# Column halves in the chunk products, transposed rows scaled once, decays made by ScalarE

## The chip, the cores and the metric

The kernel runs on one core of a Trainium2 chip. The metric is the device time of one execution in microseconds (us), lower is better. The core's engines run side by side and wait for one another through semaphores: TensorE (PE, with its weight loads shown apart as PEld), VectorE (DVE), ScalarE (ACT), GpSimd (POOL) and SyncE (SP), which here issues nearly all DMAs. PE multiplies a stationary operand (weights, `lhsT`) with a moving one and writes to banks of PSUM; DVE and ACT read these banks, POOL works on SBUF alone.

## The reference, cut to what matters

512 rows of 1024 features pass through one Mamba-2 layer, one differential attention layer and a last normalisation, all in float32. The change lies almost wholly in the first layer:

```python
h = rms_norm(x, norm_g)
zxbcdt = h @ w_in                       # z (2048), x/B/C (4096), dt (32 heads)
xbc = silu(causal_depthwise_conv(xbc, conv_w, conv_b))
dt = softplus(dt_raw + dt_bias)
a = -exp(a_log)
...
acs = cumsum(a * dt)                    # per chunk and head
seg = acs[:, :, None] - acs[:, None, :]
decay = exp(where(causal, seg, -inf))
cb = einsum("blgn,bsgn->blsg", c_c, b_c)
y_diag = einsum("blsgr,bsgrp->blgrp", cb[..., None] * decay, x_c)
y_off = einsum("blgn,bgrpn->blgrp", c_c, state) * exp(acs)
...
x = x + gated_group_rms_norm(y, z, g) @ w_out
```

There are 8 groups with 4 heads each, a head has 64 features and the state 128.

## The kernel before

**Numbers.** The large projections are made in three products of fp32r: a value is split into a head (`hi`) and a rest (`lo`), and `mm3` (L227) adds hi·hi, hi·lo and lo·hi. The gains of the norms are multiplied into the weights as they are split: ACT writes `whi` (`head`, L137), DVE `wlo` (`rest`, L143). Weights come in segments of 1 MB into `raw` (two buffers), and `whi` and `wlo` have two buffers each. The order of the segments is `order_a`, then `ORDER_B`.

**The first norm** is taken apart. The transposed rows `x_t` are split as they come (`split_x`, L356) into `hh`/`hl` ("a_hi", "a_lo" in the trace); the factor 1/rms of each row is applied later. `squares` and `scales` (L289, L294) make it as a column `r_col` (one value a row of x, for results with rows on partitions) and as a row `r_row` (copied along all partitions by a matmul of a matrix of ones with four diagonal matrices, which POOL makes). `z_out` (L344) scales by the column inside the Silu; `conv` (L471) multiplies the bank by `r_row` on DVE before its four taps.

**The groups.** For group g, `group_proj` (L485) makes four banks (B, C and two of x, 96 records of PE), each followed by `conv`: one ACT tap, three DVE taps, a Silu on ACT. `decays` (L532) fetches the cumulated sums `acs` in a DMA that repeats them over partitions, subtracts a column (POOL), fills the entries above the diagonal (POOL, `affine_select`) and takes the exponential (ACT). `ssd` (L552) makes the scores `pcb` of the group, multiplies them into the decays of each head (DVE, L582), and from these the output inside chunks `pyd` (L605: per chunk and head, `dec` as weights of 128 columns, `xdt` with 64 columns as the moving side, plain fp32), then the part from the states, gate, norm and transposes. Chunks are 128 long here.

**The order.** A planner orders the instructions of each engine by its own estimate of times, not by the order of the text. Where `Ordered.on` is set (T, A and V stand for PE, ACT and DVE), each instruction is pinned behind the one written before it on its engine. Before the change this is so for ACT and DVE in the first four tiles (L366 to L371) and in the second layer (from L687). Dense projections come from generators (`stream_a`, `stream_b`), and `until` (L281) draws from them until a step is done; so PE has projections to lay beside the chunk work.

**The end** (L986 and on) is written out by hand: the last head's transposes and gates (`gate_head`), the last projection (`rows`, L902), and residual adds put into the bank of an unfinished sum (`add_in`, L941), after which PE goes on adding to that bank.

```python
            for c in (2 * q, 2 * q + 1):
                for h in range(R):
                    o = (c % 2) * 256 + h * HD
                    T.matmul(pyd[q][:, o:o + HD], lhsT=dec[:, h, c, :], rhs=xdt[:, c, h, :], start=True, stop=True)
```

Of the kernel before, what the change touches and what calls it, by code (L numbers as in the profile page):

```python
# [17 lines left out]
P = 128  # L18
# [43 lines left out]
def trunk(ctx, tc, x, x_t, par, w_dt, w_in, w_out, w_kvqg, w_bo, d_skip, lam_qk, fin_g, out):  # L62
# [59 lines left out]
    def load(i):  # L122
# [165 lines left out]

# [5 lines left out]
    def scales(tag, ss):  # L294
# [67 lines left out]
    A.activation(begin, ident[:, 0:1], AF.Copy)  # L362
    first = load(0)()
# [7 lines left out]
    V.on = A.on = False  # L371
# [13 lines left out]
    V.tensor_scalar(out=sg1, in0=prm[:, C_SG:C_SG + 1], scalar1=0.5 * (1.0 - LAM0), scalar2=None, op0=ALU.mult)  # L385
    dtw_raw = sm.tile([P, KD, H], F32, name="dtw_raw")
    nc.sync.dma_start(dtw_raw[:], w_dt)
# [10 lines left out]
    for k in range(KD):  # L398
        w = dw[:, k].rearrange("p a b h -> p (a b h)")
        T.matmul(ps_dt, lhsT=w, rhs=hh[:, k, :], start=k == 0, stop=False)  # L400
        T.matmul(ps_dt, lhsT=w, rhs=hl[:, k, :], start=False, stop=k == KD - 1)

    pre = sm.tile([P, P], F32, name="pre")
    for c in range(NQ):
        sl, hi, lo = (slice(i * H, (i + 1) * H) for i in (c, 0, 1))
        cs = slice(c * P, (c + 1) * P)
        A.copy(pre[sl, :], ps_dt[lo, cs])
        V.tensor_tensor(out=pre[sl, :], in0=ps_dt[hi, cs], in1=pre[sl, :], op=ALU.add)
# [3 lines left out]
    V.tensor_scalar(out=pre, in0=pre, scalar1=prm[:, C_DTB:C_DTB + 1], scalar2=None, op0=ALU.add)  # L412
    e1 = sm.tile([P, P], F32, name="e1")
# [57 lines left out]
    def conv(ps, ft, name, bufs):  # L471
# [3 lines left out]

        u = ps
        V.tensor_tensor(out=u, in0=ps, in1=r_row, op=ALU.mult)
        A.activation(xc, u, AF.Identity, scale=cw[3], bias=prc[:, ft:ft + 1])
        for k in (2, 1, 0):
            d = 3 - k  # L480
            V.scalar_tensor_tensor(out=xc[:, d:], in0=u[:, :S - d], scalar=cw[k], in1=xc[:, d:], op0=ALU.mult, op1=ALU.add)
# [50 lines left out]
    def decays(j):  # L532

        for g in (2 * j, 2 * j + 1):
# [5 lines left out]
            GP.tensor_copy(een, dec[:, :, 1:3, P - 1])  # L540
            for h in range(R):
                GP.tensor_tensor(out=dec[:, h], in0=dec[:, h], in1=acs_tok[:, :, R * g + h].unsqueeze(2).to_broadcast([P, NQ, P]), op=ALU.subtract)
                GP.affine_select(out=dec[:, h], in_=dec[:, h], compare_op=ALU.is_ge, fill=-BIG, base=0,
                                 pattern=[[0, NQ], [1, P]], channel_multiplier=-1)
            decs[g] = (dec, een)
        for g in (2 * j, 2 * j + 1):
            dec, een = decs[g]
            A.activation(een, een, AF.Exp)
            for h in range(0, R, 2):
                A.activation(dec[:, h:h + 2], dec[:, h:h + 2], AF.Exp)  # L550

    def ssd(g):  # L552
# [28 lines left out]
        for h in range(R):  # L581
            V.tensor_tensor(out=dec[:, h], in0=dec[:, h], in1=pcb.rearrange("p (c l) -> p c l", l=P), op=ALU.mult)  # L582
# [319 lines left out]
    def rows():  # L902
        ws = {0: use_b(("c", 2, 0), 1, 2)}
        for t, n, hs in ((0, 0, (4, 5)), (1, 0, (4, 5)), (0, 1, (4, 5)), (1, 1, (4, 5)),
# [17 lines left out]
            elif (t, n, hs) == (2, 0, (6,)):  # L922
                add_in(t, n)
# [78 lines left out]
    gate_head(h, 0, 2)  # L1002
    turn(h, 2)
# [115 lines left out]
```

## Time and profile before

| what | us |
|---|---|
| time, median of 3 runs (lowest to highest) | 736.55 (736.23 to 737.25) |
| the profiled execution's own time | 736.51 |
| its span, first to last instruction | 734.7 |
| records of PE | 3733 |
| first record of PE starts, last one ends | 1.5, 728.1 |
| POOL busy | 114.8 |
| loads of ACT's function tables | 33, 42.3 busy |

A record is one instruction of an engine. An fp32 matmul shows as two records of PE, an fp32r one as one. Ends of PE's records are modelled, and records overlap: the distance between starts is what a record costs in a dense stretch. In rows of groups, the columns are engine, operation, tiles (written <- read), count, and lowest, middle and highest duration in ns, then first and last start; rows of the timeline give start, length, engine, line, operation, tiles, count, and in brackets the idle time before and what ended it. "L53" is the line of the helper through which PE, ACT and DVE are called, so tiles tell the instructions apart.

### The profile page before, as it was taken

The numbers are of one execution on the slowest core, as the hardware profiler recorded it, in microseconds if no ns is written. First come the engines' busy times: TensorE is split into PE (matmuls) and PEld (weight loads), VectorE is DVE, ScalarE is ACT, GpSimd is POOL, SyncE is SP. The second block draws the span as 40 slices with busy tenths as digits, with TensorE's granted clock in tenths as the row PEclk, the third lists the DMA queues.
The fourth block names the chain that finished last, engine by engine and source line by source line (L and its number), as shares of the span: only waits on it lengthen the run. The fifth ranks groups of instructions, "written<-read, shape, count | busy, mean of one in ns | idle before, by whom it ended". The sixth has DMA issues, their size and how long they took to land.

```text
span 734.7 us, 10327 instructions
## 1 busy us (share of the span) xinstructions
PE 723.1 (98%) x3733; PEld 605.0 (82%) x3733; DVE 530.8 (72%) x1202; ACT 445.3 (61%) x975; POOL 114.8 (16%) x158
## 2 busy tenths in 40 slices
PE   9999999999999999999999999999999999999996
PEld 7788878888887888877888879888898898889874
DVE  5679955798568669469895655666757857785886
ACT  6849672864829356256433258766766766766566
POOL 0117231402233141150110201000000000000002
PEclk9999999999999999999999999999999999999999
DMA  8552313224132233132113220331221131122003
GB/s 314 215 193 97 128 45 116 78 95 172 59 114 65 108 115 116 58 116 102 71 58 114 87 86 8 115 115 58 65 109 57 58 116 58 58 80 93 29 1 114
DMA packets 12914, 70.83 MB, mean 96 GB/s; under 512 B 1728, under 2 KB 2496, under 8 KB 5312
## 3 DMA queue, kind: packets, MB, share of 16 engines
q1 hardware_dynamic: 12576, 69.90, 26.5%
q8 instruction: 29, 0.48, 0.3%
q10 hardware_dynamic: 288, 0.28, 0.1%
q14 instruction: 21, 0.17, 0.1%
HBM read 68.02 MB, written 2.16 MB: 96 GB/s over the span
## 4 chain that ended last, share of the span: by engine, by line
PE 86%; DVE 6%; ACT 5%; issue 1%; DMA 1%; POOL 0%; ACTq 0%; POOLq 0%; SPq 0%
PE pg L53 20%; PE po L53 13%; PE pz L53 10%; PE pt L53 7%; PE pv L53 6%; PE pq L53 6%; PE pk L53 6%; PE pyd L53 4%; PE pb L53 3%; PE sc L53 3%; PE pc L53 2%; DVE wlo L53 2%; ACT L53 1%; PE pyt L53 1%; PE pxt L53 1%
## 5 line engine op out<-in xcount | busy, mean ns | idle before, releaser
L53 DVE SCALAR_TENSOR_TENSOR wlo<-raw,prm,whi 128x512 fp32r<-128x512 f32 (+1 forms) x256 | 151.4, 640 | 49.6 <-ACT whi L53 49.2
L53 ACT ACTIVATE whi<-raw,prm 128x512 fp32r<-128x512 f32 (+1 forms) x256 | 137.1, 609 | 58.5 <-PE pz L53 12.4
L53 PE MATMUL pg<-a_hi,whi 128*128 128x512 f32 x256 | 102.4, 401 | 0.4 <-DVE xc L53 0.4
L53 PE MATMUL pg<-a_hi,wlo 128*128 128x512 f32 x256 | 102.7, 404 | 0.0
L53 PE MATMUL pg<-a_lo,whi 128*128 128x512 f32 x256 | 101.4, 397 | 0.0
L53 DVE SCALAR_TENSOR_TENSOR xc<-pg,prc,xc 128x511 f32<-128x511 f32 (+2 forms) x96 | 70.0, 743 | 4.4 <-ACT xc L53 3.6
L53 PEld LDWEIGHTS pg<-a_hi,whi 128*128 128x128 f32 x256 | 48.2, 188 | 11.4 <-issue 0.8
L53 PEld LDWEIGHTS pg<-a_hi,wlo 128*128 128x128 f32 x256 | 48.1, 188 | 11.0
L53 PEld LDWEIGHTS pg<-a_lo,whi 128*128 128x128 f32 x256 | 48.2, 188 | 10.8
L53 PE MATMUL po<-whi,yh 128*128 128x512 f32 x128 | 50.9, 400 | 0.7 <-ACT yh L53 0.6
L53 PE MATMUL po<-wlo,yh 128*128 128x512 f32 x128 | 50.9, 400 | 0.4 <-DVE wlo L53 0.4
L53 PE MATMUL pz<-wlo,a_hi 128*128 128x512 f32 x128 | 50.5, 401 | 0.0
L53 PE MATMUL pz<-whi,a_lo 128*128 128x512 f32 x128 | 50.1, 399 | 0.0
L53 PE MATMUL po<-whi,yl 128*128 128x512 f32 x128 | 49.9, 396 | 0.0
L53 PE MATMUL pz<-whi,a_hi 128*128 128x512 f32 x128 | 49.6, 400 | 0.0
L53 ACT ACT_TABLE_LOAD x33 | 42.3, 1283 | 9.5 <-DVE xc L53 7.9
L957 POOL TENSOR_TENSOR ot<-ot,fg 128x512 f32<-128x512 f32 x4 | 5.1, 1285 | 257.6 <-PE pc L53 256.4
L53 ACT ACTIVATE s<-s,mx 128x128 f32<-128x128 f32 (+3 forms) x64 | 35.6, 559 | 9.5 <-DVE mx L53 9.3
L580 POOL TENSOR_TENSOR xe<-xdt,tok 128x256 f32<-128x256 f32 x24 | 15.4, 672 | 152.5 <-DVE xdt L53 152.5
L53 DVE CUSTOM_DVE_ANT_0 s<-sc,bias 128x128 f32<-128x128 f32 (+3 forms) x64 | 29.4, 488 | 12.3 <-PE sc L53 11.9
L53 PE MATMUL pv<-whi,b_hi 128*128 128x256 f32 x128 | 36.6, 286 | 0.0
L53 ACT ACTIVATE tmp<-dx 128x256 f32<-128x256 f32 x32 | 13.1, 411 | 38.0 <-DVE dx L53 38.0
(244 smaller groups left out, 1749.1 us busy)
## 6 DMA issues: line engine op xcount, KB each, us to landing
raw<-in_w_in SPq DMA_DIRECT2D x23, 1024.0 KB, 4.9
raw<-in_w_kvqg SPq DMA_DIRECT2D x16, 1024.0 KB, 4.8
dec<-acs_d SPq DMA_DIRECT2D x8, 1024.0 KB, 4.8
raw<-in_w_out SPq DMA_DIRECT2D x8, 1024.0 KB, 4.7
raw<-in_w_bo SPq DMA_DIRECT2D x4, 1024.0 KB, 4.8
x_tok<-in_x SPq DMA_DIRECT2D x4, 512.0 KB, 9.4
out<-ot SPq DMA_DIRECT2D x7, 256.0 KB, 2.4
raw<-in_w_in SPq DMA_DIRECT2D x4, 256.0 KB, 5.4
```

What stands on the lines that cost most here:

```text
L53: i = op(*args, **kw)
L580: GP.tensor_tensor(out=xe[:, c], in0=xdt[:, c], in1=toe_tok[:, c, hs].unsqueeze(2).to_broadcast([P, R, HD]), op=ALU.mult)
L957: GP.tensor_tensor(out=o, in0=o, in1=f, op=ALU.mult)
```

## The change

It has six parts, and computes the same outputs.

1. `pyd`: each matmul becomes two, each with 64 columns of `dec` as weights, writing partitions 0 to 63 and 64 to 127 of the bank.
2. The row of 1/rms stays in its PSUM bank. Once z0 has used the unscaled `hh`/`hl`, `xt` is multiplied by it in place and split anew (`scale_x`, `head_x`, `rest_x`); `conv` loses its multiplication, and `z_out` scales by the column for j = 0 only. The four diagonal matrices are made by DVE.
3. From the first product of z0 up to the last of `rest_x`, the order on ACT and DVE is that of the text; on PE from the first product to z0's last. The dt product moves ahead of z0's second half, `dtw_raw` is fetched where `prc` was, and `prc` later.
4. Decays: for each head and chunk, ACT takes Relu(column - value), then exp(-...), so that entries above the diagonal become 1; the exponentials of the last values (`een`) are read straight from the fetched tile.
5. The scores' bank `pcb` is multiplied by a lower triangle of ones (DVE, `ones` masked once on POOL), which takes the entries above the diagonal out.
6. At the end, `add_in(2, 0)` comes after `gate_head(h, 0, 2)`, and `add_in(3, 1)` inside `gate_head(h, 3, 4)`, ahead of its last subtraction.

```diff
@@ load
-            nc.sync.dma_start(prc[:], par[:, C_CB:N_PAR])
+            nc.sync.dma_start(dtw_raw[:], w_dt)
@@ scales
-        V.tensor_copy(col, rsqrt(ss, NT, "y"))
         w = small.tile([P, NT + 1, P], F32, tag="wide", name=f"{tag}diag", bufs=2)
         GP.memset(w[:, NT], 1.0)
+        V.tensor_copy(col, rsqrt(ss, NT, "y"))
         for t in range(NT):
-            GP.tensor_tensor(out=w[:, t], in0=ident, in1=col[:, t:t + 1].to_broadcast([P, P]), op=ALU.mult)
+            V.tensor_scalar(out=w[:, t], in0=ident, scalar1=col[:, t:t + 1], scalar2=None, op0=ALU.mult)
         ps = long_bank(f"{tag}ps_r")
-        T.matmul(ps, lhsT=w[:, NT], rhs=w[:, 0:NT].rearrange("p t n -> p (t n)"), start=True, stop=True)
-        row = res.tile([P, S], F32, tag="r_row", name=f"{tag}r_row")
-        A.copy(row, ps)
+
+        def row():
+            T.matmul(ps, lhsT=w[:, NT], rhs=w[:, 0:NT].rearrange("p t n -> p (t n)"), start=True, stop=True)
+            return ps
+
         return col, row
@@ z_out
-        A.activation(zs, ps, AF.Silu, scale=r_col[:, t:t + 1])
+        A.activation(zs, ps, AF.Silu, scale=1.0 if j else r_col[:, t:t + 1])
@@ start
-    V.on = A.on = False
+    T.on = True
     for k in range(4):
         for t in range(NT):
             tk = slice(t * P, (t + 1) * P)
             mm3(pz0[t], (hh[:, k, tk], hl[:, k, tk]), (wh[:, k, :], wl[:, k, :]), k == 0, False)
     for k in range(4, KD):
         split_x(k)
-    fetch(2)
+    second = load(1)()
     for t in range(NT):
         nc.sync.dma_start(x_tok[:, t, :], x[t * P:(t + 1) * P, :])
-    ss = sm.tile([P, NT], F32, name="ass")
-    for t in range(NT):
-        squares(ss, t)
-    r_col, r_row = scales("a", ss)
...
-    dtw_raw = sm.tile([P, KD, H], F32, name="dtw_raw")
-    nc.sync.dma_start(dtw_raw[:], w_dt)
+    third = load(2)()
+    nc.sync.dma_start(prc[:], par[:, C_CB:N_PAR])
...
         T.matmul(ps_dt, lhsT=w, rhs=hl[:, k, :], start=False, stop=k == KD - 1)
+    for piece in second:
+        lay(piece)
+    ss = sm.tile([P, NT], F32, name="ass")
+    for t in range(NT):
+        squares(ss, t)
 
     pre = sm.tile([P, P], F32, name="pre")
     for c in range(NQ):
...
+        A.copy(pre[c * H:(c + 1) * H, :], ps_dt[H:2 * H, c * P:(c + 1) * P])
+    r_col, row = scales("a", ss)
+
+    def scale_x(k):
+        V.tensor_tensor(out=xt[k // 2][:, k % 2, :], in0=xt[k // 2][:, k % 2, :], in1=r_row, op=ALU.mult)
+
+    def head_x(k):
+        A.copy(hh[:, k, :], xt[k // 2][:, k % 2, :])
+
+    def rest_x(k):
+        V.tensor_tensor(out=hl[:, k, :], in0=xt[k // 2][:, k % 2, :], in1=hh[:, k, :].bitcast(F32), op=ALU.subtract)
+
+    w0 = ready.pop(("z", 0, 1))
+    for t in range(2):
+        run(tok_mm(pz0[t], t, 1, w0))
+    r_row = row()
+    for t in range(2, NT):
+        run(tok_mm(pz0[t], t, 1, w0))
+    z_out(0, 0, pz0[0])
+    (h0, l0, _), (h1, l1, _), (h2, l2, _), (h3, l3, _) = third
+    h0(0), l0(0), h1(1)
+    scale_x(0), head_x(0), l1(1), scale_x(1)
+    h2(2), rest_x(0), z_out(0, 1, pz0[1])
+    head_x(1), scale_x(2), h3(3), rest_x(1)
+    head_x(2), l2(2), scale_x(3), z_out(0, 2, pz0[2])
+    head_x(3), rest_x(2), l3(3), rest_x(3), z_out(0, 3, pz0[3])
+    T.on = False
...
+    for k in range(4, KD):
+        scale_x(k)
+        head_x(k)
+        if k > 4:
+            rest_x(k - 1)
+    rest_x(KD - 1)
+    V.on = A.on = False
...
+    GP.affine_select(out=ones, in_=ones, compare_op=ALU.is_ge, fill=0.0, base=0, pattern=[[1, P]], channel_multiplier=-1)
...
-    w0 = use(("z", 0, 1))
-    for t in range(NT):
-        run(tok_mm(pz0[t], t, 1, w0))
-        z_out(0, t, pz0[t])
@@ conv
-        u = ps
-        V.tensor_tensor(out=u, in0=ps, in1=r_row, op=ALU.mult)
-        A.activation(xc, u, AF.Identity, scale=cw[3], bias=prc[:, ft:ft + 1])
+        A.activation(xc, ps, AF.Identity, scale=cw[3], bias=prc[:, ft:ft + 1])
@@ decays
-            GP.tensor_copy(een, dec[:, :, 1:3, P - 1])
+            A.activation(een, dec[:, :, 1:3, P - 1], AF.Exp)
             for h in range(R):
-                GP.tensor_tensor(out=dec[:, h], in0=dec[:, h], in1=acs_tok[:, :, R * g + h].unsqueeze(2).to_broadcast([P, NQ, P]), op=ALU.subtract)
-                GP.affine_select(out=dec[:, h], in_=dec[:, h], compare_op=ALU.is_ge, fill=-BIG, base=0,
-                                 pattern=[[0, NQ], [1, P]], channel_multiplier=-1)
+                for c in range(NQ):
+                    A.activation(dec[:, h, c, :], dec[:, h, c, :], AF.Relu, scale=-1.0, bias=acs_tok[:, c, R * g + h:R * g + h + 1])
+            for h in range(0, R, 2):
+                A.activation(dec[:, h:h + 2], dec[:, h:h + 2], AF.Exp, scale=-1.0)
             decs[g] = (dec, een)
...
@@ ssd
+        pcv = pcb.rearrange("p (c l) -> p c l", l=P)
+        V.tensor_tensor(out=pcv, in0=pcv, in1=ones.unsqueeze(1).to_broadcast([P, NQ, P]), op=ALU.mult)
...
-                    T.matmul(pyd[q][:, o:o + HD], lhsT=dec[:, h, c, :], rhs=xdt[:, c, h, :], start=True, stop=True)
+                    for r in (slice(0, 64), slice(64, 128)):
+                        T.matmul(pyd[q][r, o:o + HD], lhsT=dec[:, h, c, r], rhs=xdt[:, c, h, :], start=True, stop=True)
@@ end
-            elif (t, n, hs) == (2, 0, (6,)):
-                add_in(t, n)
...
     gate_head(h, 0, 2)
+    until((2, 0, 6))
+    add_in(2, 0)
     turn(h, 2)
...
-    gate_head(h, 3, 4)
+    def between():
+        until((3, 1, 5))
+        add_in(3, 1)
+
+    gate_head(h, 3, 4, between)
     square_in(2, 1)
-    until((3, 1, 5))
     rest2 = last_root(2)
     scale(1, 0, r1)
-    add_in(3, 1)
```

More of the change, by code (lines that the diff above doesn't have):

```diff
@@ L362, in trunk @@
     A.activation(begin, ident[:, 0:1], AF.Copy)
+    dtw_raw = sm.tile([P, KD, H], F32, name="dtw_raw")
     first = load(0)()
@@ L401, in trunk @@
         T.matmul(ps_dt, lhsT=w, rhs=hl[:, k, :], start=False, stop=k == KD - 1)
+    for piece in second:
[3 more added lines that the diff above has]
+        squares(ss, t)
     pre = sm.tile([P, P], F32, name="pre")
     for c in range(NQ):
[L405 to L408, printed above, removed]
+        A.copy(pre[c * H:(c + 1) * H, :], ps_dt[H:2 * H, c * P:(c + 1) * P])
[22 more added lines that the diff above has]
+    for c in range(NQ):
+        sl = slice(c * H, (c + 1) * H)
+        V.tensor_tensor(out=pre[sl, :], in0=ps_dt[0:H, c * P:(c + 1) * P], in1=pre[sl, :], op=ALU.add)
     for c in range(NQ):
@@ L412, in trunk @@
     V.tensor_scalar(out=pre, in0=pre, scalar1=prm[:, C_DTB:C_DTB + 1], scalar2=None, op0=ALU.add)
+    for k in range(4, KD):
[5 more added lines that the diff above has]
+    V.on = A.on = False
+    V.tensor_scalar(out=sg1, in0=prm[:, C_SG:C_SG + 1], scalar1=0.5 * (1.0 - LAM0), scalar2=None, op0=ALU.mult)
     e1 = sm.tile([P, P], F32, name="e1")
@@ L474, in conv @@
         cw = [prc[:, at + k:at + k + 1] for k in range(4)]
-        u = ps
-        V.tensor_tensor(out=u, in0=ps, in1=r_row, op=ALU.mult)
-        A.activation(xc, u, AF.Identity, scale=cw[3], bias=prc[:, ft:ft + 1])
+        A.activation(xc, ps, AF.Identity, scale=cw[3], bias=prc[:, ft:ft + 1])
         for k in (2, 1, 0):
             d = 3 - k
-            V.scalar_tensor_tensor(out=xc[:, d:], in0=u[:, :S - d], scalar=cw[k], in1=xc[:, d:], op0=ALU.mult, op1=ALU.add)
+            V.scalar_tensor_tensor(out=xc[:, d:], in0=ps[:, :S - d], scalar=cw[k], in1=xc[:, d:], op0=ALU.mult, op1=ALU.add)
         A.activation(xc, xc, AF.Silu)
@@ L539, in decays @@
             een = small.tile([P, R, 2], F32, tag="een", name=f"een{g}")
-            GP.tensor_copy(een, dec[:, :, 1:3, P - 1])
+            A.activation(een, dec[:, :, 1:3, P - 1], AF.Exp)
             for h in range(R):
-                GP.tensor_tensor(out=dec[:, h], in0=dec[:, h], in1=acs_tok[:, :, R * g + h].unsqueeze(2).to_broadcast([P, NQ, P]), op=ALU.subtract)
-                GP.affine_select(out=dec[:, h], in_=dec[:, h], compare_op=ALU.is_ge, fill=-BIG, base=0,
-                                 pattern=[[0, NQ], [1, P]], channel_multiplier=-1)
+                for c in range(NQ):
+                    A.activation(dec[:, h, c, :], dec[:, h, c, :], AF.Relu, scale=-1.0, bias=acs_tok[:, c, R * g + h:R * g + h + 1])
+            for h in range(0, R, 2):
+                A.activation(dec[:, h:h + 2], dec[:, h:h + 2], AF.Exp, scale=-1.0)
             decs[g] = (dec, een)
[L546 to L550, printed above, removed]
     def ssd(g):
@@ L581, in ssd @@
         for h in range(R):
-            V.tensor_tensor(out=dec[:, h], in0=dec[:, h], in1=pcb.rearrange("p (c l) -> p c l", l=P), op=ALU.mult)
+            V.tensor_tensor(out=dec[:, h], in0=dec[:, h], in1=pcv, op=ALU.mult)
         hst = bp.tile([P, 3, R, HD], F32, tag="hst", name=f"hst{g}")
```

1 line of the change is left out of this document (removed).

## The prediction

> **What bounds the kernel now.** I read the page's busy shares first, then the chain of work that ended last, then a table of stretches for the stage that the change touches most (33 to 440 us, the first layer's groups; the columns after the stretch are its length and the busy us of each engine).
>
> ```profile
> PE 723.1 (98%) x3733; PEld 605.0 (82%) x3733; DVE 530.8 (72%) x1202; ACT 445.3 (61%) x975; POOL 114.8 (16%) x158
> PE 86%; DVE 6%; ACT 5%; issue 1%; DMA 1%; POOL 0%; ACTq 0%; POOLq 0%; SPq 0%
> 33.00:60.00 27.00, 27.00 (x120) 21.73 (x119) 22.15 (x45) 16.20 (x27) 7.13 (x10) 1.00 0.43 164
> 60.00:85.00 25.00, 25.00 (x134) 21.02 (x132) 23.63 (x36) 19.47 (x28) 10.82 (x14) 1.00 0.24 85
> 85.00:106.00 21.00, 20.96 (x97) 16.59 (x95) 13.21 (x28) 13.71 (x23) 9.81 (x12) 1.00 0.27 101
> 106.00:440.00 334.00, 331.40 (x1631) 273.45 (x1631) 246.27 (x437) 175.51 (x319) 75.28 (x101) 1.00 0.27 95
> ```
>
> PE is busy for 723.1 of 734.7 us, and in the group stage it lacks 27.00 + 25.00 + 20.96 + 331.40 = 404.4 against 407: 2.6 us of visible idle. Whatever shortens DVE, ACT or POOL there can win back no more than about those 2.6 us. The time falls only if PE's own work shrinks, or if PE waits less at the two ends. So I count PE first.
>
> A busy PE can still be paying for something other than the multiplication, so I take the pitch of a record (its piece of the chain divided by its count), not its duration:
>
> ```profile
> 462.94 11.19 PE pk L53 x48
> 457.34 5.61 PE pv L53 x48
> 63.47 0.89 PE pcb L53 x8
> 76.83 1.73 PE pyd L53 x16
> L53 PEld LDWEIGHTS pyd<-xdt,dec x256: 187/192/192, 76.5 to 415.9; 128*128 128x128 f32 x128
> L53 PE MATMUL pyd<-xdt,dec x256: 217/275/275, 76.7 to 416.0; 128*128 128x64 f32 x128
> ```
>
> Moving 512 columns in fp32r costs 233 ns a record (pk), 256 columns 117 ns (pv): half. In plain fp32, where each matmul is two records, 128 moving columns cost 111 ns (pcb) and 64 cost 108 ns (pyd): not half. So pyd's 256 records pay 108 ns for something that doesn't depend on the moving side, though the moving side would need about 55. What is the same in both is the load of 128 columns of weights ahead of each record, which I take to be the price: 256 x 0.108 = 27.7 us of PE for pyd.
>
> **The change, part by part.** The sum is made against the profiled execution's 736.5 us (span 734.7 and 1.8 around it; the median of the runs shown is 736.55).
>
> *Column halves of pyd.* Each of 128 matmuls becomes two with 64 weight columns each, writing different halves of the partitions: 512 records for 256. No row of this trace has a matmul with fewer than 128 active columns, so I bound it by the rows above. Best: a half's load costs half of 108 ns and the two halves run beside one another, so a matmul takes 108 ns in place of 216: 128 x 0.108 = 13.8 us, 13.8 saved. Middle: the halves follow one another, 512 x 0.054 = 27.6, nothing saved. Worst: each half record still costs 108 ns, 512 x 0.108 = 55.3, 27.6 lost. I take the best one, since the load is what is paid and the two loads go into disjoint columns, and keep the others as rivals. Against it stands the change of the array's shape at both ends of each of the 16 stretches of pyd. The nearest rows:
>
> ```profile
> 76.67 1.89 PE L53 MATMUL pyd<-xdt,dec 128*128 128x64 f32 x16
> 78.37 0.48 PE L53 MATMUL pg<-a_hi,whi 128*128 128x512 f32 x1
> 78.68 0.40 PE L53 MATMUL pg<-a_lo,whi 128*128 128x512 f32 x1
> ```
>
> An ordinary record lasts 0.40 while its pitch is 0.23, so emptying the array exposes at most 0.17 us. Between 0 and 0.17 I take 0.10 a border: 32 x 0.10 = 3.2 us (range 0 to 5.4). Net: 13.8 - 3.2 = **10.6 us saved**.
>
> [...]
>
> *Scaling the transposed rows once, and the fixed order.* Removed: the multiplication by the row in every convolution. Added: eight scalings, eight copies, eight subtractions, and four diagonal products moved from POOL to DVE.
>
> ```profile
> L53 DVE TENSOR_TENSOR pg<-pg,ar_row x32: 685/691/700, 48.0 to 366.1; 128x512 f32<-128x512 f32 x32
> 8.75 0.76 PEld L53 LDWEIGHTS pz<-whi,a_hi 128*128 128x128 f32 x4 [0.40 <-ACT a_hi L53]
> 8.86 0.69 DVE L53 TENSOR_TENSOR a_lo<-xt,a_hi 128x512 fp32r<-128x512 f32 x1
> 12.01 2.39 ACT L53 CAST a_hi<-xt 128x512 fp32r<-128x512 f32 x4 [0.62 <-DMA xt<-in_x_t]
> 12.67 2.54 DVE L53 TENSOR_TENSOR a_lo<-xt,a_hi 128x512 fp32r<-128x512 f32 x4 [0.41 <-ACT a_hi L53]
> 16.01 1.34 ACT L53 ACTIVATE whi<-raw,prm 128x512 fp32r<-128x512 f32 x2 [1.61 <-DMA raw<-in_w_in]
> 22.65 2.02 ACT L53 ACTIVATE dw<-dtw_raw,prm 128x64 fp32r<-128x64 f32 x8
> L53 ACT ACTIVATE sq<-x_tok x4: 1044/1046/1049, 18.5 to 21.6; 128x1024 f32<-128x1024 f32 x4
> 22.78 0.17 DVE L53 TENSOR_SCALAR ass<-ass 128x4 f32<-128x4 f32 x1 [3.27 <-ACT sq L53]
> 25.59 0.17 DVE L53 COPY ar_col<-y_y 128x4 f32<-128x4 f32 x1
> L53 PE MATMUL aps_r<-adiag x2: 590/590/591, 30.3 to 30.7; 128*128 128x512 f32 x2
> 33.03 0.40 PE L53 MATMUL pg<-a_hi,whi 128*128 128x512 f32 x1
> 34.73 2.73 DVE L53 SCALAR_TENSOR_TENSOR wlo<-raw,prm,whi 128x512 fp32r<-128x512 f32 x4
> ```
>
> On DVE 32 x 0.69 = 22.1 us go and 16 x 0.635 = 10.2 come (2.54/4 a piece). PE never waited long for it in the stage, so this is costed at nothing; the cover is PE's dense projections.
>
> The new PE order has to be followed by hand from 5.7 us. The first half of z0, 48 records at 0.233 = 11.2, now in strict order, meets one new wait: a_lo of the second tile ends at 8.86 + 0.69 = 9.55, and where PE could do other products before, it now stands for some 0.4 us. End: 17.5. The dt product (16 records, 3.7) needs dw, whose ACT part follows the casts that end at 14.4 (14.4 + 2.0) and whose DVE part ends about 17.5, if its DMA, which takes prc's place in SP's queue, has landed by 14.4; prc itself moves behind two weight loads and x_tok on that queue, and is needed only in the first convolution. End: 21.2. z0's second half (t = 0, 1; 24 records) until 26.8; its weights had landed by 16.0 and are split by about 20.3. The squares follow on ACT (19.0 to 23.2), the root takes 25.76 - 22.78 = 3.0, the diagonals some 0.8: 27.0. So the matmul of the row waits 0.2 us, ends at 27.9, and t = 2, 3 end at 33.5, where the first pg started at 33.03. From 28.0 DVE has twelve steps (scale, rest of x, rest of weights, four each, 0.62 to 0.68: 7.8 us) until 35.8; PE needs the last of them at its fourth k, 33.5 + 10 x 0.233 = 35.8. So no further wait, with no margin. I put **0.6 us lost** (33.5 against 33.03, rounded up), between 0 and 2.5, the latter where every link slips by an ACT or DVE piece. Behind the waiting row matmul on PE stand the rest of z0 and g0; later k have room, as PE reaches them 48 records (11.2 us) after 33.5. The softplus chain moves back by about 6 us; PE has 22 us of the next projections to lay before it needs the decays.
>
> *Decays on ACT.*
>
> ```profile
> L542 POOL TENSOR_TENSOR dec<-dec,tok x32: 1045/1052/1497, 53.1 to 321.4; 128x512 f32<-128x512 f32 x32
> L543 POOL TENSOR_SCALAR_AFFINE_SELECT dec<-dec x32: 631/637/1090, 57.1 to 324.1; 128x512 f32<-128x512 f32 x32
> L53 ACT ACTIVATE toe<-acs x1: 405/405/405, 44.9 to 44.9; 128x128 f32<-128x128 f32 x1
> L53 DVE TENSOR_TENSOR dec<-dec,pcb x32: 676/681/689, 66.3 to 374.7; 128x512 f32<-128x512 f32 x32
> ```
>
> POOL loses 32 x (1.05 + 0.64) = 54 us that nobody on PE waited for. ACT gains 128 Relus; toe is the same form (128x128, bias from a column) at 0.405, and pieces that follow each other overlap by some 0.1 (whi above: two take 1.34, not twice 0.72), so 128 x 0.31 = 40 us. DVE gets eight masks of the scores at 0.68, 5.5 us, each ahead of the four products of its group. In the stage ACT is busy 225 of 407 us and DVE 305; they become about 265 and 290. At nothing, because PE's other projections cover; if that cover is gone it is the second rival.
>
> *The end.*
>
> ```profile
> 712.26 0.70 DVE L53 TENSOR_TENSOR pc<-pc,x_tok 128x512 f32<-128x512 f32 x1
> 712.87 0.41 DVE L53 TENSOR_TENSOR ol<-pot,oh 128x256 fp32r<-128x256 f32 x1
> 713.34 0.50 PE L53 MATMUL pc<-whi,ol 128*128 128x512 f32 x1 [0.43 <-DVE ol L53]
> 724.71 0.29 DVE L53 TENSOR_TENSOR ol<-pot,oh 128x128 fp32r<-128x128 f32 x1 [0.33 <-ACT oh L53]
> 724.98 0.69 DVE L53 TENSOR_TENSOR pc<-pc,x_tok 128x512 f32<-128x512 f32 x1
> 725.73 0.50 PE L53 MATMUL pc<-whi,oh 128*128 128x512 f32 x1 [0.44 <-DVE pc L53]
> ```
>
> At 712 the residual add stands on DVE ahead of the ol that PE waits for: moved behind it, PE's 0.43 go. At 725 PE waits for the add, which stands behind ol; moved ahead of it, DVE's idle 0.33 before ol is used and about the same is won. Together **0.8 us saved**, between 0 and 0.87.
>
> Sum: 736.5 - 10.6 + 0.6 - 0.8 = **725.7 us**.
>
> **Rivals.** *1, slower: the halves follow one another.* [...] It decides as soon as the second half's load can't start before the first half's has ended. [...] Against it: nothing in the trace; that is why it keeps a large chance.
>
> *2: ACT becomes the bound between 60 and 106 us.* ACT is busy there 19.47 + 13.71 = 33.2 of 46; the Relus of groups 0 to 3 (64 x 0.31 = 19.8) would make 53.0, 7.0 us too much, and weights are split on ACT too, so PE would stand for them: 725.7 + 7.0 = 732.7. Against: these Relus can spread into the stretches before and after (16.2 of 27 us before 60).
>
> *3: the change does not do what it says: a half costs what a whole did.* 512 x 0.108: 725.7 + 10.6 + 27.6 + 3.2 = 767.1. In this kernel it means that a half's load doesn't go beside the matmul of the other half, 54 + 54 a record. Against: PEld and PE overlap throughout, 605 beside 723 us. [...]
>
> **How the numbers follow.** Forecast 0.52 (719.5 to 731: borders at 0, 13.8 saved, 0.8 won at the end and 2.6 of idle removed give 719.3; borders at 5.4 and 2.5 lost at the start give 729.8, and some us of ACT). Rival 2 0.14, rival 1 0.22, rival 3 0.07, and 0.05 for something else, such as a schedule with new holes. About 0.2%, 1.5 us, is what a measurement of this kernel can tell from no change. Faster: 0.52 + 0.11 of rival 2 = 0.63. Within: 0.03 of rival 2, 0.06 of rival 1 (borders free), 0.02 of the rest = 0.11. Slower: 0.16 + 0.07 + 0.03 = 0.26. The range 719.5 to 741 leaves out rival 3, half of the rest and the edges. Cases of one sign hold most of the chance.
>
> **What would show it.** In the changed profile: a stretch of pyd with 32 records, about 0.9 us long plus borders (right) or 1.75 and more (rival 1), 3.5 (rival 3); the first pg at 33.5; no PE idle over 0.4 us at the two places of the end; PE's visible idle in the group stage still near 3 us and no waits of PE for whi or wlo between 60 and 110 us (rival 2 has them). The forecast is wrong above all if a pair of half records takes longer than 108 ns.

## The result and the profile after

| | us | against before |
|---|---|---|
| before, median of 4 runs | 736.59 (736.23 to 737.25) | |
| after, median of 4 runs | 749.92 (748.35 to 750.27) | 1.0176, 95% interval 1.0158 to 1.0193 |
| profiled execution after | 749.63, span 747.9 | |

The changed kernel is 13.3 us slower; 725.7 was forecast, and 741 was the upper end of the range. The page of the changed kernel, its busy shares and its chain by engine:

```profile
PE 721.2 (96%) x3989; PEld 595.1 (80%) x3989; DVE 516.6 (69%) x1198; ACT 481.6 (64%) x1108; POOL 54.6 (7%) x83
...
PE 74%; ACT 12%; DVE 8%; DMA 4%; issue 1%; SPq 0%; POOL 0%; ACTq 0%
```

The work moved in the direction that the diff says: POOL fell from 114.8 to 54.6, DVE by 14.2 (the edits account for about 5 of it, 22.1 gone and 17.3 come; its other records were shorter, and why was not tried), ACT rose by 36.3. But PE is busy only 1.9 us less than before in a span that is 13.2 longer, so it stands for 26.7 us in place of 11.6, and its part of the chain fell from 86% to 74%. The table of stretches, cut where the prediction cut it (length; busy us and records of PE, PEld, DVE, ACT, POOL; granted clock, DMA share, GB/s):

```profile
33.00:60.00 27.00, 23.47 (x103) 18.68 (x101) 24.20 (x52) 15.65 (x28) 0.30 (x1) 0.99 0.38 129
60.00:85.00 25.00, 18.36 (x79) 14.65 (x80) 13.06 (x21) 23.25 (x51) 1.76 (x3) 0.88 0.30 115
85.00:106.00 21.00, 21.00 (x150) 17.07 (x149) 18.27 (x31) 15.76 (x27) 3.55 (x5) 1.00 0.40 151
106.00:440.00 334.00, 328.46 (x1867) 264.53 (x1866) 229.12 (x427) 202.47 (x414) 39.99 (x56) 0.99 0.27 94
```

PE lacks 3.5, 6.6, 0 and 5.5 us in the four stretches, 15.7 in all, where it lacked 2.6 before. In the second, ACT is busy for 23.25 of 25 us, and the granted clock is 0.88. What PE waited for, by group (total, times, longest):

```profile
PE pg L53 <- DVE xc L53: 5.8, 1, 5.8
PE pxt L53 <- ACT xc L53: 3.2, 1, 3.2
PE psA L53 <- POOL xe L609: 2.4, 1, 2.4
PE pyt L53 <- ACT tmp L53: 2.0, 2, 1.8
```

Before, no wait in the groups was over 0.7 us. The largest stands at the second group; the timeline of ACT and then of PE there:

```profile
48.10 0.61 ACT L53 CAST a_hi<-xt 128x512 fp32r<-128x512 f32 x1
55.22 0.41 ACT L53 ACTIVATE toe<-acs 128x128 f32<-128x128 f32 x1 [6.51 <-DVE acs L53]
55.53 2.10 ACT L53 ACTIVATE xc<-pg,prc 128x512 f32<-128x512 f32 x3
...
62.29 0.76 PE L53 MATMUL pg<-a_hi,whi 128*128 128x512 f32 x1 [5.83 <-DVE xc L53]
```

ACT stands 6.5 us with `toe` at the head of its queue, because the sums `acs` come at 55.2. It stood there before the change too, for 6.0 us, but `toe` then started at 44.95 and the first tap at 48.7, in time for PE's next need of a bank at 55.7. Now the first taps of three of the first group's four convolutions stand behind it until 55.5. As long as these do not run, the group's four banks stay full, and PE has no bank for the next projection. The second group, which began at 55.7, begins at 62.3.

The sums are late by 10.3 us. DVE makes them in a chain of small steps from `q` to `acs`; here are its ends before the change, and then what stands among them after it:

```profile
38.99 0.23 DVE L53 TENSOR_SCALAR q<-e 128x128 f32<-128x128 f32 x1 [1.52 <-ACT e L53]
44.49 0.42 DVE L53 TENSOR_TENSOR_SCAN acs<-ones,adt 128x128 f32<-128x128 f32 x1
```

```profile
43.27 0.23 DVE L53 TENSOR_SCALAR q<-e 128x128 f32<-128x128 f32 x1 [0.69 <-ACT e L53]
...
47.79 1.41 DVE L53 SCALAR_TENSOR_TENSOR wlo<-raw,prm,whi 128x512 fp32r<-128x512 f32 x2
...
50.64 0.69 DVE L53 TENSOR_TENSOR a_lo<-xt,a_hi 128x512 fp32r<-128x512 f32 x1
...
54.76 0.42 DVE L53 TENSOR_TENSOR_SCAN acs<-ones,adt 128x128 f32<-128x128 f32 x1
```

The chain starts 4.3 us later, and takes 6.0 longer (11.9 for 5.9), because six pieces of the scaled rows and four weight splits now stand between its steps.

The end of this wait was not the end of its price. Table of stretches right behind it:

```profile
56.00:62.30 6.30, 0.47 (x5) 0.27 (x3) 5.97 (x10) 4.94 (x9) 0.00 (x0) 0.76 0.57 209
62.30:66.00 3.70, 3.70 (x9) 2.93 (x10) 3.70 (x6) 3.49 (x13) 0.00 (x0) 0.50 0.82 263
66.00:70.00 4.00, 4.00 (x19) 3.22 (x18) 1.50 (x3) 3.95 (x8) 0.00 (x0) 0.99 0.54 229
```

For 3.7 us after the wait the granted clock is 0.50: PE counts as busy, but does 9 records where the next 4 us have 19. So this stall cost 5.8 us and then about 1.9 more (an estimate, half of 3.7). Two others did the same: after a wait of 2.4 us at 223, and after waits of 1.8 and 0.6 at 439 to 441, the clock was 0.50 for 3.4 us each. In all PE worked 10.5 us at half the clock, some 5 us lost (an estimate, half of 10.5). This is part of why its busy time hardly fell.

And yet the halves did what they should. One stretch of `pyd` from the chain in order of time, and the Relus from the groups by line:

```profile
91.59 1.08 PE pyd L53 x32
...
L53 ACT ACTIVATE dec<-dec,tok 128x128 f32<-128x128 f32 x128 | 39.0, 390 | 0.0
```

32 records take 1.08 us where 16 took 1.73. The work was forecast well; the time was not.

### The profile page after: what moved, and what is told of

It reads as the page before. It is cut to its first block, busy times and chain, and to the rows that moved or that the text cites. A ratio compares the mean times of both kernels' runs of the same rounds, so it can differ in the third digit from the quotient of the medians.

```text
span 747.9 us, 10817 instructions
## 1 busy us (share of the span) xinstructions
PE 721.2 (96%) x3989; PEld 595.1 (80%) x3989; DVE 516.6 (69%) x1198; ACT 481.6 (64%) x1108; POOL 54.6 (7%) x83
## 4 chain that ended last, share of the span: by engine, by line
PE 74%; ACT 12%; DVE 8%; DMA 4%; issue 1%; SPq 0%; POOL 0%; ACTq 0%
PE pg L53 16%; PE po L53 14%; PE pt L53 7%; PE pv L53 6%; PE pq L53 6%; PE pk L53 6%; ACT dec L53 4%; ACT L53 3%; PE pb L53 3%; PE pz L53 3%; PE sc L53 3%; PE pc L53 2%; PE pyd L53 2%; DMA dec<-acs_d 2%; DVE wlo L53 2%; ACT whi L53 1%
## 5 line engine op out<-in xcount | busy, mean ns | idle before, releaser
L53 DVE SCALAR_TENSOR_TENSOR wlo<-raw,prm,whi 128x512 fp32r<-128x512 f32 (+1 forms) x256 | 147.7, 624 | 46.7 <-ACT whi L53 46.0
L53 PEld LDWEIGHTS pg<-a_hi,wlo 128*128 128x128 f32 x256 | 48.5, 190 | 12.3 <-DVE wlo L53 1.1
L53 PE MATMUL po<-whi,yh 128*128 128x512 f32 x128 | 52.5, 411 | 0.6 <-ACT yh L53 0.6
L53 ACT ACTIVATE dec<-dec,tok 128x128 f32<-128x128 f32 x128 | 39.0, 390 | 0.0
L53 DVE CUSTOM_DVE_ANT_0 s<-sc,bias 128x128 f32<-128x128 f32 (+3 forms) x64 | 29.4, 489 | 12.3 <-PE sc L53 11.9
L53 ACT ACTIVATE tmp<-dx 128x256 f32<-128x256 f32 x32 | 13.2, 412 | 36.4 <-DVE dx L53 36.4
L53 PE MATMUL pv<-wlo,b_hi 128*128 128x256 f32 x128 | 35.7, 279 | 0.0
```

The source lines that it names most:

```text
L53: i = op(*args, **kw)
```

## The experiments

At first there were two theories: A, what was costed at nothing (the late sums, ACT's Relus) ends on PE's path; B, the halves do not save. The first four runs (3 rounds each, as all but one below) took the parts singly. "Before" beside them was 736.9 to 737.7 in all runs.

**e1: part 1 alone.**

```diff
-                    T.matmul(pyd[q][:, o:o + HD], lhsT=dec[:, h, c, :], ...)
+                    for r in (slice(0, 64), slice(64, 128)):
+                        T.matmul(pyd[q][r, o:o + HD], lhsT=dec[:, h, c, r], ...)
```

> The kernel before with part 1 alone (column halves of pyd). Theory A (the stalls of the changed kernel come from the other parts, the halves only shorten PE's work): pyd's stretches take 1.08 us for 32 records, as in the changed kernel, against 1.73 before, 16 x 0.65 = 10.4 us less, so 726 us (725 to 728). Theory B (the halves are part of the loss: shorter chunk work leaves PE less to lay, so it stands elsewhere for as long): 733 to 738.

744.9 us, ratio 1.0106 (1.0077 to 1.0136). Both theories missed: slower than before, though a stretch of `pyd` takes 1.08 here too. PE's largest wait is one that nobody expected:

```profile
PE po L53 <- DVE x_tok L53: 6.6, 1, 6.6
```

An output projection waits 6.6 us for a residual add on DVE, which the edit does not touch.

**e2: parts 4 and 5 alone** (and nothing else).

```diff
-                GP.tensor_tensor(out=dec[:, h], in0=dec[:, h], in1=acs_tok..., op=ALU.subtract)
-                GP.affine_select(out=dec[:, h], ...)
+                for c in range(NQ):
+                    A.activation(dec[:, h, c, :], dec[:, h, c, :], AF.Relu, scale=-1.0, bias=acs_tok...)
...
+        V.tensor_tensor(out=pcv, in0=pcv, in1=ones..., op=ALU.mult)
```

> The kernel before with parts 4 and 5 alone (decays on ACT, mask on the scores). Theory A (ACT now has what POOL did, and its queue stands for the decays' DMA and for 16 Relus at a time ahead of convolutions): slower than before, by 5 to 12 us, 742 to 749. Theory B (only the late softplus chain of part 3 makes the decays hurt): within 3 us of before, 734 to 740.

750.6 us, 1.0183 (1.0158 to 1.0209): B is out, and it is 1.6 more than A allowed. PE waits most for POOL's `xe` (6.1 us in four waits).

**e3: parts 2 and 3 alone.**

```diff
-        V.tensor_tensor(out=u, in0=ps, in1=r_row, op=ALU.mult)
+        V.tensor_tensor(out=xt[k // 2][:, k % 2, :], in0=xt[k // 2][:, k % 2, :], in1=r_row, op=ALU.mult)
...
-    V.on = A.on = False
+    T.on = True
```

> The kernel before with parts 2 and 3 alone (rows scaled once, fixed order). Theory A (the cumulated sums are ready at 55 us in place of 45, ACT's toe waits for them at the head of ACT's queue with the convolutions of the first group behind it, PE stands some 6 us near 56 us): slower by 4 to 8 us, 741 to 745. Theory B (the late sums hurt only because the decays that follow them are on ACT): within 2 us of before.

753.3 us, 1.0225 (1.0197 to 1.0252): more than the whole change loses, and outside both ranges. A's wait is there (5.5 us for `xc` at the second group), but others follow that A did not have (2.4, 2.2 and 1.5 us).

**e4: the change without part 1** (the diff of e1 taken back).

```diff
-                    for r in (slice(0, 64), slice(64, 128)):
+                    T.matmul(pyd[q][:, o:o + HD], lhsT=dec[:, h, c, :], ...)
```

> The changed kernel without part 1. Theory A (halves save 10.4 us of PE whatever is around them): 760 us (758 to 762). Theory B (what the halves save is lost again in waits): 750 to 754.

753.5 us, 1.0223 (1.0205 to 1.024), as B expected. The halves are worth 3.6 us there.

The three groups of parts lose 7.9, 13.6 and 16.3 us by themselves, 37.8, but 13.3 together. Costs that belonged to the edits, each by itself, would add up. So I formed theory C: *every edit makes the planner lay the rest of the program anew; the order of the kernel before is one in which PE hardly ever stands, and the new ones are not.* By the names of their tiles, PE's rows without `pyd` stand in e1 as before for the first tenth (367 of 3477); behind that another row stands in 671 places, and on DVE in 257 of 1186. To test C, order and work have to be parted.

**e5: the halves in the old order.** Each instruction is tied behind its predecessor in a list of places, engine by engine; only the order of issue is fixed by this, the waits for data stay as they are. The list is the old order, with two halves in the place of one product (128 products, 512 records as halves).

```diff
+    for e, text in packed.items():
+        at, last = 0, None
+        for step in zlib.decompress(base64.b64decode(text)).decode().split():
+            at += int(step)
+            if last is not None:
+                tc.add_manual_dep(mine[e][at], last.name, mybir.DependencyInfo(mybir.DependencyClass.NoSync, ...), reason="pin")
+            last = mine[e][at]
```

> The products in column halves (part 1 alone), with every engine's instructions held in the order of the kernel before: each of the 512 products is replaced in its place by its two halves, and nothing else stands elsewhere than before. In e1 the same products were laid in a new order and took 744.9. Theory C (the halves save what was forecast, and the new order lost it): 726 us, 724 to 729. Rival (the halves themselves cost, by their borders or by a mode of the array that slows their neighbours): 735 to 746, that is not below the kernel before by more than 2.

**730.4 us** (729.8 to 730.65), ratio 0.9905 (0.9889 to 0.9921): faster than both kernels, though not the 726 of C. Timeline of PE, first of before, then of e5:

```profile
76.23 0.59 PE L53 MATMUL psB<-xe,bt 128*128 128x256 f32 x2
```

```profile
77.22 0.59 PE L53 MATMUL psB<-xe,bt 128*128 128x256 f32 x2
77.75 1.15 PE L53 MATMUL pyd<-xdt,dec 128*64 128x64 f32 x32
78.83 0.50 PE L53 MATMUL pg<-a_hi,whi 128*128 128x512 f32 x1
```

With the prediction's rows (`pyd` at 76.67, `pg` at 78.37), a stretch went from 1.70 to 1.08, and the step into it from 0.44 to 0.53: 0.53 net, 8.5 us for 16. PE's waits in the groups add up to 3.9 us in place of 2.4, which takes back the rest.

**e6: nothing changed but the order.** Whole products, held in e1's order (same code, another list).

```diff
-        trunk(tc, *args, o)
+        trunk(tc, *args, o); pin(tc, PLANNED)
```

> The kernel before with nothing changed in its work, whole products included, but every engine's instructions held in the order that e1 had. Theory C (the order loses): slower than the kernel before by what the order costs, e1's 744.9 plus the saving of the halves where no wait hides it: 748 to 756. Rival (the halves themselves cost and the order is as good): 735 to 739.

752.0 us, 1.0193 (1.0172 to 1.0214). C holds for this part: the order alone costs 14.2. (By their traces, e6 has e1's order on every engine, and e5 that of before.) Timeline of DVE, then of PE:

```profile
234.79 2.46 DVE L53 TENSOR_TENSOR dec<-dec,pcb 128x512 f32<-128x512 f32 x4
237.18 1.40 DVE L53 SCALAR_TENSOR_TENSOR wlo<-raw,prm,whi 128x512 fp32r<-128x512 f32 x2
238.51 0.73 DVE L53 SCALAR_TENSOR_TENSOR xc<-pg,prc,xc 128x510 f32<-128x510 f32 x1
239.17 0.15 DVE L53 TENSOR_SCALAR y_y<-y_i 128x4 int32<-128x4 int32 x1
239.23 1.40 DVE L53 SCALAR_TENSOR_TENSOR wlo<-raw,prm,whi 128x512 fp32r<-128x512 f32 x2
240.56 0.73 DVE L53 SCALAR_TENSOR_TENSOR xc<-pg,prc,xc 128x511 f32<-128x511 f32 x1
241.22 1.27 DVE L53 TENSOR_TENSOR x_tok<-po,x_tok 128x512 f32<-128x512 f32 x2
...
241.94 0.79 PE L53 MATMUL po<-whi,yh 128*128 128x512 f32 x1 [6.86 <-DVE x_tok L53]
```

PE's last product ended at 235.1, but the `x_tok` add that empties its bank stands behind some 6 us of decays, weight splits and convolution taps in DVE's queue. No one of these is late by itself; they stand in front. The stretch after it has the low clock again:

```profile
242.00:249.00 7.00, 7.00 (x23) 5.57 (x24) 4.06 (x12) 4.03 (x7) 0.00 (x0) 0.75 0.35 142
249.00:256.00 7.00, 7.00 (x37) 5.87 (x36) 5.23 (x8) 3.89 (x7) 0.00 (x0) 1.00 0.26 87
```

**e7: parts 4 and 5 in the old order**, the Relus right ahead of their exponential (the diff of e2, and the list).

```diff
+        trunk(tc, *args, o); pin(tc, PLANNED)
```

> Parts 4 and 5 alone (decays by ScalarE, mask in the scores' bank), every engine held in the order of the kernel before; the 16 Relus of a pair of decays stand on ACT right ahead of the exponential that they feed, the mask's product on DVE right ahead of the first product with the decays. In its own new order (e2) this work took 750.6. Theory C (the loss is the new order's): 734 to 739. Rival (the Relus' own time: blocks of 16 x 0.31 = 5 us in ACT's queue hold up the convolutions and their banks): 742 to 752.

766.5 us, 1.0402 (1.0384 to 1.0421). Here C falls: the old order is the worse one for this work. Timeline of ACT, then of PE:

```profile
106.02 4.79 ACT L53 ACTIVATE dec<-dec,tok 128x128 f32<-128x128 f32 x16
110.71 1.99 ACT L53 ACTIVATE dec<-dec 128x1024 f32<-128x1024 f32 x2
112.71 1.28 ACT L53 ACT_TABLE_LOAD   x1
114.01 0.69 ACT L53 ACTIVATE zs<-pz,ar_col 128x512 f32<-128x512 f32 x1
114.59 1.70 ACT L53 ACTIVATE tmp<-dx,y_y 128x256 f32<-128x256 f32 x4
...
115.14 2.10 PE L53 MATMUL pyt<-ident,tmp 128*128 128x128 f32 x8 [4.11 <-ACT tmp L53]
```

A block of 4.8 us stands ahead of the gate's `tmp`, and PE's transposes wait 4.1 us for it. PE waits 13.2 us for `tmp` in five such waits; the first group's `pyd` is 6.0 us late (82.7 for 76.7), the last one's 28.7.

**e8: parts 2 and 3, the groups in the old order** (the diff of e3, and the list from the first group on).

```diff
+        trunk(tc, *args, o); pin(tc, PLANNED)
```

> Parts 2 and 3 alone (rows scaled once, fixed order at the start), the instructions from the first group on held in the order of the kernel before, the start as in e3. In its own new order (e3) it took 753.3, with the second group 6.5 late. Theory C: the start's own loss stays and no more comes, 739 to 744. Rival (the edits cost by themselves all through the groups): 747 to 754. Should the late sums be the planner's doing alone: 734 to 738.

742.3 us, 1.0062 (1.0046 to 1.0078): of e3's 16 us, 11 were the order's. The second group is 6.9 late (6.5 in e3), and from there on nothing more is lost.

**e9: all six parts, the groups in the old order** (the changed kernel, and the list).

```diff
+        trunk(tc, *args, o); pin(tc, PLANNED)
```

> All six parts, the instructions from the first group up to the last stage held in the order of the kernel before (halves in the place of their product, Relus ahead of their exponential, mask ahead of the first product); start and last stage as the planner lays them. Theory C: 736.5 less 7 for the halves, plus some 6 at the start and 1 at the end, 733 to 739. Rival (the edits cost by themselves): 745 to 752, as the changed kernel.

759.3 us, 1.0297 (1.027 to 1.0325): both ranges missed. PE waits 12.3 us for `tmp` in five waits, as in e7 (13.2); what the decays cost here is read off against e13 below.

**e10: e5 with part 6**, all before the last stage in the old order.

```diff
+    def between():
+        until((3, 1, 5))
+        add_in(3, 1)
```

> e5 with part 6 (the sums into the accumulators moved, at the end): all before the last stage held in the order of the kernel before, the last stage as the planner lays it. If part 6 saves the forecast 0.8: 729.0 to 730.0, beside 730.4 of e5. If its place only moves the wait (as the wait of 1.0 for DVE's pc in the changed kernel suggests): 730.5 to 732.

731.7 us, 0.9929 (0.9911 to 0.9947), beside 730.4: the intervals overlap, so undecided by itself.

**e11: the mask alone** (part 5), POOL going on as before, in the old order.

```diff
+        V.tensor_tensor(out=pcv, in0=pcv, in1=ones..., op=ALU.mult)
```

> Part 5 alone in the order of the kernel before: the mask's 8 products in the scores' bank (8 x 0.69 us of DVE), each ahead of the group's first product with the decays, while POOL goes on subtracting and selecting as before (so the mask is applied twice). e7 with the Relus too took 766.5. If the Relus in ACT's queue cost it all: 736 to 739. If the mask's wait on DVE, between the scores and the products, carries a share: 742 to 752.

737.8 us, 1.0001 (0.9991 to 1.0011). The mask is free; e7's loss is the Relus'. The run also shows that holding an order costs nothing by itself: but for the mask its rows stand as in the kernel before.

**e12: half the Relus.**

```diff
-            for h in range(R):
+            for h in range(2, R):
                 for c in range(NQ):
                     A.activation(dec[:, h, c, :], dec[:, h, c, :], AF.Relu, ...)
```

> As e7, but with half the Relus: heads 0 and 1 of each group by POOL as before, heads 2 and 3 by 8 Relus on ACT (8 x 0.31 = 2.4 us a group) right ahead of their exponential; the mask in the bank for all. If every microsecond of Relus in that place is on PE's path (no slack): about half of e7's loss, 749 to 754. If ACT has slack there and only the longer block outlasts it: 738 to 745.

749.8 us, 1.0153 (1.0126 to 1.0181). None: free, half: about 11 us, all: 29. In that place ACT has little slack, and less the longer the block: 20 us of Relus (64 x 0.31) cost some 11, and the next 20 some 18.

**e13 and e14: the change without the decays**, in the old order and in the planner's own (parts 4 and 5 of the diff taken back).

```diff
-                    A.activation(dec[:, h, c, :], dec[:, h, c, :], AF.Relu, ...)
+                GP.affine_select(out=dec[:, h], ...)
```

> The changed kernel without parts 4 and 5 (decays by POOL as before), the groups held in the order of the kernel before. By addition of e5 and e8: 737.3 - 7 (halves) + 5 (start) = 735.4, so 734 to 738; the distance to e9's 759.3, some 23, is then the Relus' in the old order. If the parts hinder one another even in this order: 741 or more.

735.6 us, 0.9981 (0.9972 to 0.999). In a held order the parts add up: 7 won, 5 lost (part 6, at the end, is in it too).

> The same kernel as e13 in the order that the planner makes for it. If the re-laid order loses by itself, as it did with e6 (14.6) and e3 against e8 (11): 744 to 752. If what the changed kernel lost is the Relus' alone: 734 to 738, as e13.

748.9 us, 1.0164 (1.0148 to 1.018). Same work, another order: 13.2 us.

**e15: part 6 alone** (5 rounds).

```diff
-            elif (t, n, hs) == (2, 0, (6,)):
-                add_in(t, n)
...
+    until((2, 0, 6))
+    add_in(2, 0)
```

> Part 6 alone: the planner's order for it differs from that of the kernel before only among the last 5% of each engine's instructions. Forecast of step (d): 0.8 less, 736.3 to 736.9 beside 737.4. If the place of the sums only moves the wait to another product: 737 to 738.5.

738.9 us, 1.0029 (1.0017 to 1.0041): slower. Timeline of PE at the end:

```profile
712.87 0.50 PE L53 MATMUL pc<-whi,oh 128*128 128x512 f32 x1 [0.51 <-ACT oh L53]
...
724.19 0.50 PE L53 MATMUL pc<-whi,oh 128*128 128x512 f32 x1 [0.99 <-DVE pc L53]
```

The waits of 0.43 and 0.44 became 0.51 and 0.99, but they are not the same waits. DVE's timeline, a row of before, then of e15:

```profile
721.33 0.69 DVE L53 TENSOR_TENSOR pc<-pc,x_tok 128x512 f32<-128x512 f32 x1
```

```profile
723.45 0.69 DVE L53 TENSOR_TENSOR pc<-pc,x_tok 128x512 f32<-128x512 f32 x1
...
726.71 0.70 DVE L53 TENSOR_TENSOR pc<-pc,x_tok 128x512 f32<-128x512 f32 x1 [0.21 <-PE pc L53]
727.32 0.28 DVE L53 TENSOR_TENSOR ol<-pot,oh 128x128 fp32r<-128x128 f32 x1
```

The last add, `add_in(3, 1)`, does stand ahead of `ol` now (726.71), and PE stands only 0.09 us for it: that half came as forecast. The 0.99 is for another add, `add_in(2, 1)` (723.45), which has the same neighbours on DVE as before the change (721.33). What changed is PE's order: its projections now run six products ahead of its other work, so that between `po` and the product that needs this add nine stood before (720.0 to 722.0) and three stand now. Probably the `until` that moved with the first add draws them early; this is read from the code and was not tried. At the first place DVE still has the add ahead of `ol` (712.39 and 713.07), so nothing was won, and PE waits for `oh` from ACT. In the trace 1.0 us is lost here, and 0.7 before it, where the program is the same.

**e16: e8 with the last row's rounding (ACT) and remainder (DVE) ahead of four splits of a later weight**; everything else as in e8. The order of DVE:

```diff
+ a_lo<-xt,a_hi
  wlo<-raw,prm,whi x2
  q<-q
  wlo<-raw,prm,whi x2
- a_lo<-xt,a_hi
```

> e8 (rows scaled once, groups in the old order) with one instruction moved on DVE and one on ACT: the last row's rounding and its remainder, which stood behind four splits of a later weight, ahead of them. In e8 PE stood 3.3 us for remainders at 46 to 51 and then had a clock of 0.65 to 0.79 for 12 us, and the second group came 6.9 late. If that wait carries the start's loss: 736 to 738.5. If the late sums (the softplus chain and what follows on ACT) carry it: 741 to 743.

739.7 us, 1.0036 (1.0022 to 1.005): between the two ranges, nearly half of e8's loss gone. PE's waits at this place, of e8 and of e16:

```profile
PE pg L53 <- DVE a_lo L53: 3.0, 3, 2.1
```

```profile
PE pg L53 <- DVE a_lo L53: 1.0, 3, 0.6
```

Two us less of waiting made the second layer (its first `pv`) start 2.9 earlier (452.5 for 455.4): the low clock behind the wait went too, while other waits grew by 1.4 (`ps_tt` for `toe` 0.8, `pyt` for `tmp` 0.6). Stretches of e8, then of e16:

```profile
48.00:54.00 6.00, 3.67 (x9) 2.67 (x10) 5.18 (x13) 0.93 (x2) 0.00 (x0) 0.65 0.44 154
54.00:60.00 6.00, 6.00 (x22) 4.79 (x21) 4.98 (x11) 2.95 (x4) 0.00 (x0) 0.79 0.10 34
```

```profile
48.00:54.00 6.00, 5.95 (x25) 4.68 (x26) 5.86 (x15) 3.96 (x7) 0.00 (x0) 1.00 0.24 57
```

What was measured, work against order (us):

| work | old order | order that the planner makes for it |
|---|---|---|
| before | 737.7 | 752.0 (e1's order, e6) |
| halves | **730.4** (e5) | 744.9 (e1) |
| rows scaled once, start | 742.3 (e8) | 753.3 (e3) |
| decays on ACT, mask | 766.5 (e7) | 750.6 (e2) |
| all but the decays | 735.6 (e13) | 748.9 (e14) |
| all | 759.3 (e9) | 749.9 (after) |

Read along the rows: the made order loses 11 to 15 us for all work without the new decays, and wins 9 to 16 for the work with them. Read down: the halves win 7 in either order (737.7 to 730.4, 752.0 to 744.9). The decays lose 24 on top of the other parts in the old order, and 1 in the made one. So the changed kernel's 13.3 us are 1.3 won by the work without the decays (e13), 13.2 lost by the order made for it (e14), and 1.0 by the decays, 13 in sum.

## Why the prediction was wrong

**The step that failed.** The sum 736.5 - 10.6 + 0.6 - 0.8 has no term for the order: it costs what moves to DVE and ACT "at nothing", covered by PE's projections, and leaves every other instruction where it stood. In its place the runs show 13.2 us: 735.6 for all parts but the decays in the held order (e13), 748.9 for the same work in the order made for it (e14). In the trace of the changed kernel this is 15.1 us more of standing and some 5 of slow clock (the estimate from 10.5 us at 0.50), against the 8.5 that `pyd` gives: some 12 of the 13.3.

**What bounds the kernel** held: PE was full in the groups, and only PE's own work and its waits could move the time. What it left out is that this fullness was a property of one order, which the edits to the first layer gave up wherever the planner laid them.

**Halves** (10.6 saved): right in kind, the two halves run side by side. Rivals 1 and 3 are out, since a stretch of 32 half records takes 1.08 us where 16 whole ones took 1.73, not as much or more. The size was 2 us too large: a stretch, its exit counted, became 0.62 shorter, 10 in all, and the step into it cost 0.09, so 8.5 were won there against 10.6 forecast, and 7 in the time. The 3.2 us for 32 borders were my estimate from a record's 0.40 and its pitch of 0.23; no run shows the array emptying at a border, and what e5 shows is the 0.09 of the step in (0.53 for 0.44). A pair of half records takes 58 ns, where 54 were forecast and 108 named as the bound. By the starts of the changed kernel's records the halves of a pair begin 6 to 7 ns apart in most pairs, their weight loads too, with all of them on the same 128 rows.

**The start** (0.6 lost): the first `pg` came at 33.6 for the forecast 33.5. The link that failed here stands two sentences on: "The softplus chain moves back by about 6 us; PE has 22 us of the next projections". It moved back by 10 (`toe` from 44.95 to 55.22), and the 22 us were not to be had: the projections need banks, and the banks are emptied by ACT and DVE, whose queues held the late sums. I counted PE's work and not what it needs. And DVE's 22.1 us less lay in the groups, where nobody waited for them, while the 10.2 more lay at 29 to 51, in the way of the sums. In the held order it is the remainders themselves that PE waits for (3.0 us in e8; the changed kernel has no such wait): e8 measured 5 us for the start, and e16 that about 2 of these hang on one remainder behind four splits.

**Decays** ("At nothing, because PE's other projections cover"): in the changed kernel's own order they cost 1.0 (e14), but that sets two made orders against each other and does not show the cover. In the old order, held fixed, they cost 24 (e9 against e13), and e11 and e12 put this on the Relus in ACT's queue. ACT's 39.0 us were forecast as 40; the mistake was to see room for them in a mean of 225 of 407 us. There they stand in the one place where the gate, the convolutions and PE wait for ACT in turn. Rival 2 named the mechanism but shut it into 60 to 106 us and priced it at 7. Its sign, PE waiting for `whi` or `wlo` there, did not come; ACT was nearly full from 60 to 85 (23.25 of 25 us), and PE waited for its `xc` (3.2 and 1.1).

**The end** (0.8 saved): wrong in sign, 1 to 2 lost (e15, and 1.3 by e10 against e5, undecided). The second half was right: the add came ahead of `ol`, and its wait went from 0.44 to 0.09. In the first the planner left the add ahead of `ol`, and PE waited for `oh` next. And the reading followed DVE's rows alone: PE's projections came to run six products ahead, so that another add lost its cover, 0.99.

**The case that came true** got 0.05, "something else, such as a schedule with new holes". All four edits to the first layer that the planner was left to lay (e1, e2, e3, e14) came out 8 to 16 us above the kernel before; even the halves, which won 7 us in the old order, came out 8 slower (e1). Why the planner's made orders come out worse than the old one is not settled; that it lays instructions by estimated times is known from the kernel, but which estimates are off was not tried. Nor was an order tried that lets the Relus go at no cost, nor a third buffer for the decays.

## What to carry to other kernels

If a planner orders the program, an edit is two changes, its work and a new order, and the second can be larger: hold the old order fixed, measure the work, and only then let go of it; here that turns a loss of 8 us into a gain of 7 for the halves alone. In ACT's queue a busy share of 61% did not mean room, as half the Relus cost some 11 us there (e12): ask what stands behind the new instructions at that place, and whose bank or buffer it empties. And count with a stall of PE the slow microseconds after it, here 3.7 at a clock of 0.50 behind a wait of 5.8.

## What the runs showed of the hardware that was not expected

- In the changed kernel, after a wait of 5.8 us, PE's granted clock was 0.50 for 3.7 us, and by the starts of its records fp32r products of 512 columns came 427 ns apart in place of 233; a wait of 2.4 us at 223 in the same run was followed by 0.50 for 3.4 us, and in e8, where PE started six records between 45.0 and 50.8 and no single wait was over 2.1 us, the clock was 0.50 from 50 to 56.
- In the changed kernel two half-column records with the same rows start 6 to 7 ns apart in most pairs, and a pair comes every 58 ns where a whole record came every 112 before; entering the half-column form cost 0.09 us (e5).
